# A list schedule with another order of dense tiles and other ranks, a gate taken chunk by chunk, and a tail in pairs

## The chip, the cores and the metric

The kernel runs on 1 core of one Trainium2 chip. The metric is the device time of one execution in microseconds (us); before the change it is 1162.19 us, the median of 3 runs (1161.91 to 1167.45). The engines are named as the profile names them: PE (TensorE), DVE (VectorE), ACT (ScalarE), POOL (GpSimd) and SP (SyncE, which here issues the DMAs).

## The reference, cut to what matters

Two layers work on 128 context tokens and 512 latent tokens of width 1024, all in float32. Layer 0 is a Conformer convolution branch, which the change does not touch. Layer 1 is a bidirectional Mamba-2 branch, and a final RMSNorm follows:

```python
u = h @ w_in
z, xbc, dt_raw = jnp.split(u, [SSD_INNER, SSD_INNER + XBC_DIM], axis=-1)
xbc = jax.nn.silu(depthwise_conv(xbc, w_conv, b_conv))
xs, bm, cm = jnp.split(xbc, [SSD_INNER, SSD_INNER + SSD_GROUPS * D_STATE], axis=-1)
dt_f = jax.nn.softplus(dtr_f + dt_bias_f.astype(f32))
...
y_f, s_f = ssd_scan(xs, dt_f, a_f, bm, cm, h0_f)
y_b, s_b = ssd_scan(flip(xs), flip(dt_b), a_b, flip(bm), flip(cm), h0_b)
y = y_f + flip(y_b) + d_skip.astype(f32)[:, None] * xs.astype(f32)
y = y.reshape(b, l, SSD_INNER) * jax.nn.silu(z.astype(f32))
y = rms_norm(y.reshape(b, l, SSD_GROUPS, SSD_INNER // SSD_GROUPS),
             norm_g.reshape(SSD_GROUPS, SSD_INNER // SSD_GROUPS)).reshape(b, l, SSD_INNER)
return y.astype(h.dtype) @ w_out, s_f, s_b
```

The scan runs in chunks of 128 tokens: chunk 0 holds the context tokens, chunks 1 to 4 the latent ones. The 32 heads lie in 4 groups, and the norm is taken over each group of 512 channels.

## The kernel before

Channels lie on the 128 partitions and the 640 tokens along a row. The tokens stand in two sides of 320 (64 of context and 256 of latent tokens each). Everything the change touches is in layer 1, and it is issued by a list scheduler written in the kernel, the class `Order`. Each piece of work is a Python generator, a chain, which yields operations with an engine and an assumed duration (`op`, `either`), waits for named results (`key`) or waits for a free buffer of a ring (`get`). At each step `run` takes the operation that could start earliest by the assumed clocks; ties go to the lower rank `prio`, then to the older chain. So the instruction order of all five engines is fixed when the program is built. On the chip each engine goes through its own row in that order and waits at semaphores.

**Dense tiles.** A projection tile is 8 k-blocks x 3 products (high and low halves of weights and activations) in two token halves, 48 matmuls. Its weights come by one DMA (`w_load`, L782), are rounded on ACT (`wh`, L786), and the remainder `wl` is made on DVE or POOL, whichever `either` favours (L790). Tiles are named here by letter, group and number. `x` tiles (16), `b` and `c` tiles (4 each) need the short convolution (`convolve`): the product leaves PSUM through one of two `up` buffers, then DVE makes four multiply-adds (L856) into one of three `xs` (or two `bc`) buffers, ACT takes the SiLU, and PE transposes into tokens (`to_tokens`, L879) in one of two `xt` buffers. `z` tiles (16) leave PSUM by ACT alone (L932) into the single `zs` buffer of their group. `o` tiles are the output products of groups 0 to 2 (`out2`). The tile products share two PSUM slots, `mm`. The chain `filler` takes the tiles in one fixed list; before, that list is x02 x03 b0 c0 x10 to x13, then group by group z tiles, b, c, x and o tiles, and the last group's products at the end.

**Groups.** `time_steps` turns the raw dt into softplus by a polynomial and into running sums, on DVE (L1391, L1394). `group` then runs the scan of a group chunk by chunk, in the order 4, 3, 2, 1, 0 (the last group 4, 3, 0, 2, 1): decays by DMA, POOL and DVE (`decay_half`), states (`chunk_state`), products (`py`, L1154), and y with the single `y` buffer, brought back to channels on PE (`pty`, L1113) and added on DVE (L1117). `norm` waits for all chunks of y, multiplies by the SiLU of z in 16 small DVE products per group (L1186), squares on ACT (L1197), sums on PE, takes the reciprocal root, scales (L1231) and splits into halves (`split_y`). Only then is the group's `zs` buffer free, and the group's `o` tiles can start.

**Tail.** The last group is normalised side by side (side 1 first). `last_products` makes 8 column tiles per side of 12 matmuls, each in its own `mm` slot; `last_residual` adds on DVE (L1280), squares on ACT and adds the squares up on DVE (L1290). `final` sums over the partitions (L177), takes root and reciprocal, spreads the result (L182), scales into `fo` buffers on DVE (L1331), and stores (L1336).

## Time and profile before

| | us |
|---|---|
| median of 3 runs (lowest, highest) | 1162.19 (1161.91, 1167.45) |
| the profiled execution | 1166.93 |
| its span, first to last instruction | 1165.0 |
| PE busy | 1083.9 |
| DVE busy | 845.9 |
| POOL busy | 562.9 |
| ACT busy | 557.7 |
| mean granted PE clock | 0.971 |

Layer 1's dense tiles start at about 595 us of the span. "Busy" counts an engine's instructions from start to end; a busy PE is one with a matmul in flight. In the rows of a timeline or of the chain, `x48` merges equal neighbours, the first number is the start and the second the time that the merged rows cover, and a bracket tells how long the engine stood idle before and what ended that. In a windows view, PEclk is the share of full speed that PE's clock was granted.

### The profile page before, as it was taken

How to read it: one execution, taken by the hardware profiler on the slowest of the kernel's cores; microseconds unless marked ns; L12 is line 12 of the kernel's file. 1: busy time of each engine (PE TensorE's matmuls, PEld its weight loads, DVE VectorE, ACT ScalarE, POOL GpSimd, SP SyncE). 2: the span in 40 equal slices, each digit the busy share in tenths (PEclk: the TensorE clock that was granted, in tenths of full speed). 3: DMA queues.
4: the chain of work that ended last, by engine and by line, in shares of the span. 5: the costliest groups of instructions: out<-in, count | busy, mean ns of one | idle time of the engine just before them, and what ended most of it. 6: DMA issues, size and time to landing. Idle time of an engine off the chain costs nothing. (4 is left out here: it accounts for less than half of the span.)

```text
span 1165.0 us, 18976 instructions
## 1 busy us (share of the span) xinstructions
PE 1083.9 (93%) x7548; PEld 985.5 (85%) x7548; DVE 845.9 (73%) x1234; ACT 557.7 (48%) x877; POOL 562.9 (48%) x467
## 2 busy tenths in 40 slices
PE   6999999998999999999986999988999999999886
PEld 3898888888998999999886978866899889988666
DVE  2588999899989499314768785798656975575776
ACT  6534447455554456212645655373257433562331
POOL 2156779777878448000020576626551565237410
PEclk9999999998998999999997999989999999999988
DMA  9343423341222112514222443423433343324202
GB/s 363 144 127 127 136 83 112 126 137 54 98 66 62 55 46 68 172 52 136 73 76 61 134 124 109 123 64 96 125 94 106 93 113 109 119 82 133 75 1 91
DMA packets 79047, 121.21 MB, mean 104 GB/s; under 512 B 5488, under 2 KB 49008, under 8 KB 78960
## 3 DMA queue, kind: packets, MB, share of 16 engines
q1 hardware_dynamic: 78960, 120.01, 32.9%
q8 instruction: 59, 0.97, 0.4%
q14 instruction: 28, 0.23, 0.1%
HBM read 115.07 MB, written 4.92 MB: 103 GB/s over the span
## 5 line engine op out<-in xcount | busy, mean ns | idle before, releaser
L361 DVE SCALAR_TENSOR_TENSOR cva<-v,cst,cva 128x550 f32<-128x550 f32 (+12 forms) x386 | 285.9, 814 | 10.2 <-ACT cva L354 8.7
L80 POOL TENSOR_TENSOR wl<-wf,wh 128x1024 fp32r<-128x1024 f32 (+1 forms) x50 | 119.1, 2383 | 124.8 <-ACT wh L78 120.0
L78 ACT CAST wh<-wf 128x1024 fp32r<-128x1024 f32 (+1 forms) x75 | 71.4, 955 | 185.1 <-PE o__4929 L148 37.4
L390 POOL TENSOR_TENSOR cv<-cv,tp 128x490 f32<-128x490 f32 (+3 forms) x94 | 113.7, 1213 | 13.7 <-ACT cv L388 9.4
L786 ACT CAST wh<-wf 128x1024 fp32r<-128x1024 f32 x53 | 55.6, 1048 | 97.6 <-issue 27.9
L824 PE MATMUL o<-yhl,wh 128*128 128x320 f32 x384 | 98.9, 345 | 0.0
L790 DVE TENSOR_TENSOR wl<-wf,wh 128x1024 fp32r<-128x1024 f32 x49 | 70.0, 1428 | 29.1 <-ACT wh L786 29.0
L824 PE MATMUL pz<-h_hi,wh 128*128 128x384 f32 (+1 forms) x256 | 88.4, 345 | 1.2 <-ACT zs L933 1.2
L385 ACT ACTIVATE tp<-v,cst 128x490 f32<-128x490 f32 (+3 forms) x94 | 65.7, 715 | 40.7 <-POOL cv L390 40.6
L1094 POOL TENSOR_TENSOR y<-y,yo 128x512 f32<-128x512 f32 x32 | 48.6, 1518 | 67.6 <-DVE yo L1092 67.5
L824 PE MATMUL pz<-h_hi,wl 128*128 128x384 f32 (+1 forms) x256 | 79.2, 309 | 0.0
L824 PE MATMUL pz<-h_lo,wh 128*128 128x384 f32 (+1 forms) x256 | 79.1, 309 | 0.0
L824 PEld LDWEIGHTS o<-yhl,wh 128*128 128x128 f32 x384 | 66.2, 192 | 13.6 <-issue 13.3
L824 PE MATMUL xs<-h_hi,wh 128*128 128x384 f32 (+1 forms) x224 | 73.3, 327 | 4.8 <-ACT up L843 4.8
L856 DVE SCALAR_TENSOR_TENSOR xs<-up,cst,xs 128x642 f32<-128x642 f32 x64 | 72.4, 1136 | 6.2 <-ACT xs L854 5.3
L80 DVE TENSOR_TENSOR wl<-wf,wh 128x512 fp32r<-128x512 f32 (+1 forms) x25 | 27.2, 1086 | 67.6 <-ACT wh L78 67.5
L969 POOL TENSOR_TENSOR gb<-gb,cols 128x512 f32<-128x512 f32 x40 | 48.5, 1212 | 45.8 <-DMA gb<-acd 36.4
L824 PE MATMUL xs<-h_hi,wl 128*128 128x384 f32 (+1 forms) x224 | 70.0, 312 | 0.0
L824 PE MATMUL xs<-h_lo,wh 128*128 128x384 f32 (+1 forms) x224 | 69.9, 312 | 0.0
L969 POOL TENSOR_TENSOR gf<-gf,cols 128x512 f32<-128x512 f32 x40 | 51.5, 1288 | 36.1 <-DMA gf<-acd 36.1
L824 PE MATMUL o<-yhl,wl 128*128 128x320 f32 x192 | 60.2, 314 | 0.0
L628 POOL MEMSET up<- 128x2 f32 x2 | 0.2, 100 | 118.5 <-DVE h_lo L219 118.5
(678 smaller groups left out, 3469.4 us busy)
## 6 DMA issues: line engine op xcount, KB each, us to landing
wf<-w_in SPq DMA_DIRECT2D x48, 512.0 KB, 3.6
wa<-w_ada SPq DMA_DIRECT2D x64, 256.0 KB, 4.7
wf<-w_out SPq DMA_DIRECT2D x24, 512.0 KB, 3.7
wf<-w_xbc SPq DMA_DIRECT2D x24, 512.0 KB, 3.7
gf<-acd SPq DMA_DIRECT2D x40, 256.0 KB, 4.6
gb<-acd SPq DMA_DIRECT2D x40, 256.0 KB, 4.5
wa<-w_ada SPq DMA_DIRECT2D x16, 512.0 KB, 9.9
wf<-w_z SPq DMA_DIRECT2D x16, 512.0 KB, 3.8
```

Of the source, the lines that this page charges most:

```text
L78: S.copy(out=wh[:, :n], in_=wf[:, :n])
L80: sub.tensor_sub(out=wl[:, :n], in0=wf[:, :n], in1=wh[:, :n].bitcast(F32))
L361: V.scalar_tensor_tensor(out=rows(acc)[:, :, lo:hi], in0=rows(v)[:, :, lo + d : hi + d], scalar=w_dw(i, tap), in1=rows(acc)[:, :, lo:hi], ...
L385: S.activation(out=tp[:, :, 0 : hi - lo], in_=rows(v)[:, :, lo + d : hi + d], func=AF.Copy, scale=w_dw(i, tap))
L390: G.tensor_add(out=rows(out)[:, :, lo:hi], in0=rows(out)[:, :, lo:hi], in1=tp[:, :, 0 : hi - lo])
L628: G.memset(t[:, 0:2], 0.0)
L786: S.copy(out=cell["wh"], in_=cell["wf"])
L790: e_.tensor_sub(out=cell["wl"], in0=cell["wf"], in1=cell["wh"].bitcast(F32))
L824: T.matmul(ps[:, b, at_ : at_ + t1 - t0], lhsT=w_, rhs=t_[:, t0:t1], start=k == 0 and n == 0, stop=k == nk - 1 and n == 2)
L856: t = yield op(VE, 0.95, lambda: V.scalar_tensor_tensor(out=acc, in0=u[:, d : d + PW], scalar=c("w_c", j * 5 + d), in1=acc, op0=ALU.mult, ...
L969: yield op(PO, 1.15, lambda: G.tensor_sub(out=gt, in0=gt, in1=cols1[ch][:, o : o + 4].unsqueeze(2).broadcast_to([P, 4, 128])))
L1094: t = yield op(PO, 1.35, lambda: G.tensor_add(out=y, in0=y, in1=yo))
```

## The change

- **Order of the tiles.** The list of `filler` is written out as a string, `PLAN`. `z` tiles stand early and between the `x` tiles: z00 first, then x02, b0, c0, x10, x03, z01 and so on. The `x` tiles of groups 2 and 3 and the `o` tiles are spread.
- **Ranks.** `start` takes its rank from a table by the chain's name, `PRIO`, in place of a number at each call. `either` gets its own bias in place of a common one, and an `up` buffer is taken by the time at which it came free, not in turn.
- **Gate by chunk.** The 16 products of `norm` become one product per chunk and group (L1191 of the changed kernel, 5 per group, 512 elements each), in chains of their own, `gate`, which start as soon as the chunk's y and the four z tiles are there. The squares may go to ACT or to DVE.
- **y buffers.** From the third chunk of the last group on, y has two further buffers, which come free when the last projection tile is done.
- **Tail.** Two column tiles share one `mm` slot; the last products wait for the residuals of group 2 and are chains with ranks of their own. The squares of columns 1 to 5 are added up on POOL, and those of columns 6 and 7 go to the partition sum as they are. `final` works in three overlapping parts of 128 tokens (one root, one reciprocal), scales in place in `x` and stores from there.
- **Series.** In `time_steps` the factors 1/17 and 2 of the polynomial are moved into the multiply-adds, and two TENSOR_SCALAR instructions are gone. The logarithm starts earlier in the chain.

```diff
-                            key = (t + 0.4 * load if len(ch[4][1]) == 1 else t + dur - 1.25 + 2.0 * n, ch[2], ch[3])
+                            key = (t + 0.4 * load if len(ways) == 1 else t + dur - ways[0][1] + bias * n, ch[2], ch[3])
...
+        PRIO = {"x_after": 2, "filler": 3, "decay_half": 3, "decay_state": 1, "chain0": 0, "chain1": 0, "other_y": -3, "copy_y": -1, "split_y": -1, "groups": 0, "decays": -1, "norms": -3, "gate": 3, "products1": 3, "products0": 2, "residual0": 1, "final0": -2, "w_chain": 0, "time_steps": 1, "columns": 0, "logarithm": 0, "rows_out": 0, "ends_out": 1, "weights_out": 0, "first_steps": 0, "b_after": -2, "c_after": 0, "z_after": 2, "split": 3, "add_residual": 2, "out_weights": 1, "free_bc": -1, "final1": 3, "prompt": -3, "residual1": 0, "store": -1}
...
-            u = up[ups[0] % 2]
-            ups[0] += 1
+            ups.sort()
+            u = up[ups.pop(0)[1]]
...
+                ring = "y" if g < 3 or n < 2 else "y3"
+                yield get(ring)
...
+        def gate(g, ch):
+            yield key(("y", g, ch), *[("z", g, j) for j in range(4)])
+            zv = halves4(grp[g]["zt"])
+            zv = zv[:, :, :, 0:64] if ch == 0 else zv[:, :, (ch - 1) // 2, 64 + (ch - 1) % 2 * 128 : 192 + (ch - 1) % 2 * 128]
+            yv = grp[g]["xt"][:, ch, :]
+            yv = yv.rearrange("p (j b n) -> p j b n", j=4, b=2) if ch == 0 else yv.rearrange("p (j n) -> p j n", j=4)
+            t = yield op(VE, 0.68, lambda: V.tensor_mul(out=zv, in0=zv, in1=yv))
+            post(("gate", g, ch), t)
...
-            yield key(*[("y", g, ch) for ch in chs])
+            yield key(*[("gate", g, ch) for ch in chs])
...
-                t = yield op(VE, 0.45, lambda: V.tensor_add(out=accs[b][0], in0=accs[b][0], in1=sq))
-                put("xs", t)
+                t = yield op(PO, 0.85, lambda: G.tensor_add(out=accs[b][0], in0=accs[b][0], in1=sq))
+                put(nm, t)
...
-        PARTS = ((0, 128), (128, 128), (256, 64))
+        PARTS = ((0, 128), (128, 128), (192, 128))
...
-                yield get("st")
-                o = lp.tile([P, 512], F32, tag="st", bufs=6, name="fo")[:, 0:HN]
-                t = yield op(VE, 0.5, lambda: V.scalar_tensor_tensor(out=o, in0=x[k][:, tok], scalar=c("fg", k), in1=cell[0], op0=ALU.mult, op1=ALU.mult))
-                start(store(k, tok, o), t, 1)
+                t = yield op(VE, 0.54, lambda: V.scalar_tensor_tensor(out=x[k][:, tok], in0=x[k][:, tok], scalar=c("fg", k), in1=cell[0], op0=ALU.mult, op1=ALU.mult))
+                start(store(k, tok), t)
...
+        PLAN = "z00 x02 b0 c0 x10 x03 z01 x11 x12 z02 b1 x20 x21 z03 x13 x30 x22 x31 c1 z10 b2 z11 x23 x32 c2 o00 o01 o02 x33 z12 z13 o03 b3 z20 z21 o10 c3 o11 z22 z23 o12 z30 o13 z31 o20 z32 z33 o21 o22 o23"
...
-            yield tts(0.36, V.tensor_scalar, out=u, in0=t, scalar1=1.0 / 17, scalar2=None, op0=ALU.mult)
             for n in (15, 13, 11, 9, 7, 5, 3):
-                yield stt_(out=u, in0=u, scalar=1.0 / n, in1=t, op0=ALU.add, op1=ALU.mult)
-            yield tts(0.36, V.tensor_scalar, out=u, in0=u, scalar1=1.0, scalar2=2.0, op0=ALU.add, op1=ALU.mult)
-            yield tts(0.5, V.tensor_mul, out=q, in0=q, in1=u)
+                yield stt_(out=u, in0=t if n == 15 else u, scalar=17.0 / n, in1=t, op0=ALU.add, op1=ALU.mult)
+            yield stt_(out=q, in0=u, scalar=17.0, in1=q, op0=ALU.add, op1=ALU.mult)
```

What the change moves is seen in the order of the instructions on each engine. The first place is the start of layer 1's tiles on PE: `pt<-cst,v` are the transposes of the end product v of `time_steps`, `xs` and `B` are tiles. Before:

```order
L824 MATMUL xs<-h_lo,wh 128x256
L824 MATMUL xs<-h_hi,wl 128x256
L1462 MATMUL pt<-cst,v 128x128 x3
L1462 MATMUL pt<-cst,t 128x128 x3
L824 MATMUL B<-h_hi,wh 128x384
L824 MATMUL B<-h_lo,wh 128x384
```

And now, at the same transposes:

```order
L827 MATMUL B<-h_hi,wh 128x256
L827 MATMUL B<-h_lo,wh 128x256
L827 MATMUL B<-h_hi,wl 128x256
L1460 MATMUL pt<-cst,v 128x128 x3
L827 MATMUL B<-h_hi,wh 128x256
```

Ahead of the transposes of v stood two tiles (x02, x03); now two tiles (z00, x02) and 30 of b0's 48 matmuls stand there. On DVE, the polynomial at the same place, before:

```order
L1394 TENSOR_SCALAR q<-e 128x384
L1394 RECIPROCAL q<-q 128x384
L1394 TENSOR_TENSOR t<-e,q 128x384
L1394 TENSOR_TENSOR t<-t 128x384
L1394 TENSOR_SCALAR u<-t 128x384
L1391 SCALAR_TENSOR_TENSOR u<-u,t 128x384 x7
L1394 TENSOR_SCALAR u<-u 128x384
L1394 TENSOR_TENSOR q<-q,u 128x384
```

and now:

```order
L1396 TENSOR_SCALAR q<-e 128x384
L1396 RECIPROCAL q<-q 128x384
L1396 TENSOR_TENSOR t<-e,q 128x384
L1396 TENSOR_TENSOR t<-t 128x384
L1393 SCALAR_TENSOR_TENSOR u<-t 128x384
L1393 SCALAR_TENSOR_TENSOR u<-u,t 128x384 x6
L1393 SCALAR_TENSOR_TENSOR q<-u,q 128x384
```

The two TENSOR_SCALAR rows on u are gone. Beside this chain POOL makes the remainders `wl` of the next tiles' weights: three of them before the first decay before, five now; DVE made two just ahead of it before, one now.

The second place is DVE after the last chunks of group 0's y (`xt<-xt,pty`). Before, the convolution of B and C stands around the gate `zs<-zs,xt`, whose 16 rows follow each other (four of them shown):

```order
L790 TENSOR_TENSOR wl<-wf,wh 128x1024
L856 SCALAR_TENSOR_TENSOR C<-up_5971,cst,C 128x642 x2
L970 COPY_PREDICATED gf<-msk,gb 128x512
L1117 TENSOR_TENSOR xt<-xt,pty 128x512
L856 SCALAR_TENSOR_TENSOR B<-up_5967,cst,B 128x642
L1186 TENSOR_TENSOR zs<-zs,xt 128x64
L1186 TENSOR_TENSOR zs<-zs,xt 128x256
L1186 TENSOR_TENSOR zs<-zs,xt 128x64
L1186 TENSOR_TENSOR zs<-zs,xt 128x256
```

and now, where three of the five gate rows already stand further up:

```order
L1133 TENSOR_TENSOR xt<-xt,pty 128x512
L1161 TENSOR_TENSOR gf<-gf,pcb 128x512
L869 SCALAR_TENSOR_TENSOR xs<-up_5971,cst,xs 128x642 x4
L869 SCALAR_TENSOR_TENSOR B<-up_5967,cst,B 128x642 x3
L1133 TENSOR_TENSOR xt<-xt,pty 128x512
L869 SCALAR_TENSOR_TENSOR B<-up_5967,cst,B 128x642
L1191 TENSOR_TENSOR zs<-zs,xt 128x8x64
L1191 TENSOR_TENSOR zs<-zs,xt 128x4x128
L793 TENSOR_TENSOR wl<-wf,wh 128x1024
```

Between the last y of group 0 and the first y of group 1, DVE had 22 rows of convolution (16 for x, 4 for B, 2 for C), 16 of gate and 4 remainders; it now has 13 (8, 1, 4), 2 and 5. PE had 246 dense matmuls there and now has 267.

The third place is the end of PE's row: `o` are the last products, `rps<-ones,sq` the sums of squares, `rps<-cst,rc` the spreading. Before:

```order
L1308 MATMUL o_11246<-yhl,wh_10896 128x320 x2
L1308 MATMUL o_11246<-yhl,wl_10897 128x320
L177 MATMUL rps<-ones,sq 128x1 x4
L177 MATMUL rps<-ones,sq 64x1 x2
L182 MATMUL rps<-cst,rc 128x128 x2
L182 MATMUL rps<-cst,rc 128x64
```

and now:

```order
L1329 MATMUL o_11136<-yhl,wl_10959 128x320
L1329 MATMUL o_11136<-yhl,wh_10958 128x320 x2
L1329 MATMUL o_11136<-yhl,wl_10959 128x320
L177 MATMUL rps<-ones,sq 128x1 x18
L182 MATMUL rps<-cst,rc 128x128 x6
```

Side 1's sums, spread and scaling stood among side 0's products; now those of both sides stand behind the last product, and DVE scales and SP stores all 16 pieces after it. Further up in the tail, 120 dense matmuls stand between the last y that side 1 needs and its first product (48 before), and 135 between the last y of side 0 and its first product (90 before).

More of the change, by code (lines that the diff above doesn't have):

```diff
@@ L753, in op, with either @@
             return "op", ((eng, dur, fn, table),)
[L755 to L756 removed]
+        def either(*ways, bias=2.0):
+            return "op", tuple((e_, d_, f_, None) for e_, d_, f_ in ways), bias
         def key(*ks):
@@ L802, in w_load @@
             t = yield op(SP, 0.1, load)
-            start(split(), t, 1)
+            start(split(), t)
         W = {}
@@ L1323, in final @@
-            for p, cols in ((P, slice(0, 2)), (64, slice(2, 3))):
-                yield op(ACT, 0.26, lambda: S.activation(out=rc[0:p, cols], in_=ps[0:p, 384:387][:, cols], func=AF.Sqrt, scale=1.0 / 1024, bias=epsb[0:p]), "sqrt")
-                yield op(VE, 0.16, lambda: V.reciprocal(out=rc[0:p, cols], in_=rc[0:p, cols]))
+            t = yield op(PE, 1.0, lambda: column_sums(ps[:, 384:387], accs[b], PARTS))
+            for _ in range(3):
+                put(SQ[b][0], t)
+            rc = gp.tile([P, 3], F32, tag="rc", bufs=1, name="rc")
@@ L1326, in final @@
+            yield op(ACT, 0.26, lambda: S.activation(out=rc, in_=ps[:, 384:387], func=AF.Sqrt, scale=1.0 / 1024, bias=epsb), "sqrt")
+            yield op(VE, 0.16, lambda: V.reciprocal(out=rc, in_=rc))
             cell = []
```

224 lines of the change are left out of this document (104 added, 120 removed).

## The prediction

> **What bounds the kernel now.** First the page's head and its row of engines:
>
> ```profile
> span 1165.0 us, 18976 instructions
> PE 1083.9 (93%) x7548; PEld 985.5 (85%) x7548; DVE 845.9 (73%) x1234; ACT 557.7 (48%) x877; POOL 562.9 (48%) x467
> ```
>
> PE is busy for 93% of the span, so the question is where the other 7% lie. The change touches layer 1, from 595 us on; the windows view cuts that into stretches (length, then busy time of PE, PEld, DVE, ACT, POOL, then granted clock, DMA share, GB/s):
>
> ```profile
> 595.00:640.00 45.00, 32.29 (x197) 31.15 (x196) 39.68 (x53) 22.37 (x37) 8.92 (x4) 0.81 0.28 82
> 640.00:740.00 100.00, 98.87 (x661) 88.76 (x659) 72.86 (x87) 58.59 (x86) 63.99 (x46) 1.00 0.42 123
> 740.00:815.00 75.00, 63.83 (x412) 54.72 (x411) 66.82 (x93) 39.65 (x68) 38.62 (x29) 0.91 0.30 90
> 815.00:1085.00 270.00, 268.40 (x1827) 242.33 (x1826) 177.39 (x283) 121.29 (x189) 129.06 (x105) 1.00 0.37 108
> 1085.00:1154.00 69.00, 58.86 (x362) 48.46 (x360) 50.56 (x115) 24.90 (x47) 15.29 (x11) 0.93 0.13 40
> 1154.00:1165.00 11.00, 2.42 (x18) 2.09 (x18) 5.13 (x13) 0.87 (x3) 0.00 (x0) 0.70 0.34 119
> ```
>
> In 640 to 740 and 815 to 1085 PE idles 1.1 + 1.6 = 2.7 of 370 us at full clock: nothing to gain. PE loses in three places: the start (idle 12.7, clock 0.81), the change from group 0 to 1 (idle 11.2, clock 0.91) and the tail (idle 10.1, clock 0.93), and behind the last product come 11 us with little PE work. A low clock stretches work: (1 - 0.81) x 45 = 8.6, 0.09 x 75 = 6.8 and 0.07 x 69 = 4.8 us. The list of waits names who ends PE's idle time there (us, times, longest):
>
> ```profile
> PE pt L1462 <- DVE v L1394: 11.3, 1, 11.3
> PE py L1154 <- DVE gf L1145: 4.2, 3, 2.7
> PE xs L824 <- ACT up L843: 3.5, 1, 3.5
> PE rms L1221 <- DVE rq L1213: 3.3, 1, 3.3
> PE rms L1207 <- ACT ysq L1197: 1.9, 2, 1.0
> PE o L1308 <- DVE x L1280: 1.9, 3, 0.8
> ```
>
> So DVE, at 89% in the second stretch (66.82 of 75), is late while PE has nothing else in its row.
>
> **Start.** PE's timeline around the one long wait, and a whole tile from the chain:
>
> ```profile
> 608.61 0.28 PE L824 MATMUL xs<-h_hi,wl 128*128 128x256 f32 x1
> 620.19 0.88 PE L1462 MATMUL pt<-cst,v 128*128 128x128 f32 x3 [11.30 <-DVE v L1394]
> 621.74 0.90 PE L1462 MATMUL pt<-cst,t 128*128 128x128 f32 x3 [0.67 <-DVE t L1452]
> 623.38 0.69 PE L824 MATMUL B<-h_hi,wh 128*128 128x384 f32 x1 [0.73 <-ACT up L843]
> 1001.56 7.03 PE B L824 x48
> ```
>
> Of b0's 48 matmuls 30 now stand ahead of v's transposes: 30/48 x 7.03 = 4.4 us of work that fills part of the 11.3. A tile is a tile, so z00 in place of x03 is nothing by itself; but a z tile needs no `up` buffer, so B's wait of 0.73 for ACT's move into `up` goes; I leave the 0.67 for t. The shorter idle time also costs less low clock. Against this stands when v is ready. DVE's and POOL's timelines:
>
> ```profile
> 599.20 0.35 DVE L1394 TENSOR_SCALAR q<-e 128x384 f32<-128x384 f32 x1
> 603.36 2.44 DVE L1394 TENSOR_SCALAR u<-t 128x384 f32<-128x384 f32 x1
> 605.83 4.11 DVE L1391 SCALAR_TENSOR_TENSOR u<-u,t 128x384 f32<-128x384 f32 x7
> 609.98 2.50 DVE L1394 TENSOR_SCALAR u<-u 128x384 f32<-128x384 f32 x1
> 619.49 0.56 DVE L1394 TENSOR_TENSOR v<-rp,v 128x384 f32<-128x384 f32 x1
> ```
>
> ```profile
> 602.91 2.67 POOL L790 TENSOR_TENSOR wl<-wf,wh 128x1024 fp32r<-128x1024 f32 x1 [0.76 <-ACT wh L786]
> 609.93 2.34 POOL L790 TENSOR_TENSOR wl<-wf,wh 128x1024 fp32r<-128x1024 f32 x1 [4.35 <-ACT wh L786]
> ```
>
> The two instructions that go took 2.44 + 2.50, yet their sister of the same size took 0.35. Each ended just after a remainder on POOL: 605.80 after 605.58, 612.48 after 612.27. So 2 x 2.1 of their 4.9 us were time under POOL, and their own worth is 0.7. If the next instruction is held in their stead, v comes 0.7 earlier; if none is, 4.9 (2.44 + 2.50). POOL now makes five remainders there, not three, so v can also come later, by one or two more such blocks of 2.1; DVE makes one remainder less. I take v as before: gain 4.4 + 0.7 and 0.9 for the clock = **6**, with bounds 2 (two more blocks) and 15 (4.9 earlier, and half of the low clock's 8.6 back).
>
> The Trainium skill, "SBUF — State Buffer", section "Who interferes with whom", says that a DVE instruction with two SBUF inputs contends with a GpSimd instruction that reads SBUF, and that the holder blocks the other for its whole duration. By that rule the multiply-adds, whose inputs are both in SBUF, would be held like the scalar steps, and the larger number of remainders on POOL would speak against the change. The trace agrees for the two 2.4 us rows. By that rule the time would be that of the second rival below, not that of the sum.
>
> **Group 0 to group 1.** DVE's timeline from the last gate to the last split, with the groups by line over layer 1 and a later 128x512 product of that kind:
>
> ```profile
> 747.63 8.61 DVE L1186 TENSOR_TENSOR zs<-zs,xt 128x64 f32<-128x64 f32 x16
> 756.17 0.88 DVE L856 SCALAR_TENSOR_TENSOR B<-up,cst,B 128x642 f32<-128x642 f32 x1
> ...
> 795.51 0.48 DVE L1244 TENSOR_TENSOR yhl<-zs,yhl 128x320 fp32r<-128x320 f32 x1
> ...
> 814.36 0.69 DVE L1117 TENSOR_TENSOR xt<-xt,pty 128x512 f32<-128x512 f32 x1
> ```
>
> ```profile
> L856 DVE SCALAR_TENSOR_TENSOR xs<-up,cst,xs 128x642 f32<-128x642 f32 x64 | 72.4, 1136 | 6.2 <-ACT xs L854 5.3
> L790 DVE TENSOR_TENSOR wl<-wf,wh 128x1024 fp32r<-128x1024 f32 x48 | 68.7, 1432 | 28.7 <-ACT wh L786 28.5
> ```
>
> The old gate held DVE for 8.6 us in one piece. Now five products, at 0.69 by the 128x512 row: 3.4, three of them earlier. Between the last y of group 0 and the first y of group 1 DVE loses 9 convolution rows (9 x 1.14 = 10.2), 14 gate rows (8.61 - 2 x 0.69 = 7.2) and gains one remainder (1.4): **16 us less work**, where PE was idle or slowed for 11.2 + 6.8 = 18. PE's own row gains 21 dense matmuls there (21/48 x 7.03 = 3.1), which are work taken from elsewhere, and cover. Since the shortfall and the relief are alike, I take **15**; bounds 5 (only the 4.2 of `gf` and the low clock that it brings go) and 18 (all).
>
> **Tail.** PE waits there for `rq`, `ysq` and x: 3.3 + 1.9 + 1.9 = 7.1 of the idle 10.1. Between the last y and the first product of side 1 stand 120 dense matmuls in place of 48, of side 0 135 in place of 90: 72/48 x 7.03 = 10.5 and 6.6 us more cover, over norm chains whose waits are 3.3 and 1.9. Tiles in pairs leave DVE two tiles' time per slot, so the 1.9 for x go. Those 7.1, 1.1 of the remaining idle 3.0, and the low clock's 4.8 make **13**; bounds 6 (only `rq` and the pairs' half) and 15.
>
> **End.** After the last product:
>
> ```profile
> 1153.67 0.31 PE L1308 MATMUL o<-yhl,wl 128*128 128x320 f32 x1
> 1154.61 0.48 DVE L1290 TENSOR_TENSOR sq<-sq 128x320 f32<-128x320 f32 x1
> 1155.14 1.38 PE L177 MATMUL rps<-ones,sq 128*128 128x1 f32 x12 [1.17 <-DVE sq L1290]
> 1157.16 1.04 PE L182 MATMUL rps<-cst,rc 128*128 128x128 f32 x6 [0.64 <-DVE rc L1325]
> 1158.24 3.76 DVE L1331 SCALAR_TENSOR_TENSOR fo<-x,cst,rps 128x320 f32<-128x320 f32 x8 [1.09 <-PE rps L182]
> 1158.82 3.78 SPq L1336 DMA_DIRECT2D o_y<-fo  x8
> ```
>
> (The trace counts two records for one of these matmuls.) 6 sums took 1.38; 18 take 4.1, of which 1.2 fit into PE's wait for the residual and 0.5 replaces the last add: +1.1. Eight more scalings and stores at 3.78/8 follow one another: +3.8. The second side's spread hides behind the first side's scaling. **Cost 5**, bounds 3 (all sums hidden) and 7 (none, and the spread too). The adds of squares on POOL have no row: at least the 0.48 of DVE's, at most the 2.67 of a remainder three times as long. At five or six per side, 32 us at most, beside POOL's 15.29 busy of 69, they cost nothing while products cover them; the last two columns skip the add.
>
> The remaining edits (choice of `up` buffer, `either`'s bias, further y buffers) show only in the order just counted. Their risk is new stalls in the 370 full us; PE has 2.7 us of idle time there, and DVE's 72.86 in 100 and 177.39 in 270 leave it room, so I put it at 0, up to 5.
>
> **Sum.** 6 + 15 + 13 - 5 = 29. The profiled execution's own time is 1166.9, 4.7 above the median; 1166.9 - 29 = 1138 stands for a run like it, and 1162.2 - 29 = **1133** for the median, which I predict. A difference of 0.5%, 5.8 us, is about what a measurement of this kernel can tell from no change.
>
> **Rivals.**
>
> *v is not held* (0.13). The removed steps were the ones that POOL's remainders caught; if the multiply-adds slip through, the start gains 15: 1133 - 9 = 1124. For: the seven took 4.11, 0.59 each, though part of one remainder's span lay near. Against: five remainders in place of three.
>
> *POOL holds DVE more* (0.17). Layer 1 gives POOL six more remainders and ten adds of squares. v comes two blocks later (start 2), and half the relief between the groups is eaten: 1133 + 4 + 7.5 = 1145. For: the two 2.4 us rows. Against: 6 x 2.1 = 13 us over the whole layer, most of it where DVE has slack. (The Trainium skill's rule quoted above leads here.)
>
> *Nothing gained* (0.08). The idle time only moves to the next late piece: gains under 10 us before the end's cost of 5, so 1157 to 1168. For: DVE's 89% in the second stretch; against: its work falls there.
>
> *Slower* (0.08). Group 1's first two z tiles now stand among group 0's; the next two need the single `zs` buffer only when norm has split group 0, and each occupies one of two `mm` slots until ACT moves it out. If the split is late, both slots are held and PE starves. From group 0's last y to there PE has 228 dense matmuls (33.4 us) and about 8 of other work, 42 us; before, the last gate to the last split took 756.2 to 796.0 = 39.8. With the 16 us of relief the split needs some 24, so it would decide only beyond 42; each us beyond is lost at three group changes. At 58 us (16 over, 48 lost, 29 gained) the time is 1181.
>
> **How the numbers follow.** Forecast (1126 to 1141) 0.54, v not held 0.13, POOL holds 0.17, nothing gained 0.08, slower 0.08. Low: all upper bounds, 6 → 15, 15 → 18, 13 → 15 and 5 → 3, make 45 or 1117; a little beyond, 1114, as the groups 1 to 3 may gain too. High: 2 + 5 + 6 - 7 = 6 gives 1156; I end at 1154, leaving out the cases without a gain. Faster by over 0.5% is the first three cases and a part of the fourth's edge: 0.85; within 0.5% 0.07; slower 0.08.
>
> **What would show it.** Right: PE's gap before `pt<-cst,v` is near 6 us; no window between 720 and 800 has a clock under 0.95; PE's waits for `rq`, `ysq` and x are under 2 us together; from the last product to the end 15 to 16 us, with 16 stores in a row. Wrong: v's last product later than 20.3 us after `q<-e` (619.49 - 599.20 before); long multiply-adds beside POOL's remainders; a wait of `pz` for ACT's move into `zs`, which would be the slower case; or new idle time in the full stretches.

## The result, and the profile after

The changed kernel takes 1145.32 us (median of 4 runs, 1144.77 to 1151.12) beside 1163.55 us for the kernel before: a ratio of 0.985, with a 95% interval from 0.9808 to 0.9892. Forecast were 1133 us and a range from 1114 to 1154. The time lies in the range and fell as forecast, but by 18 us in place of 29.

To see where the 18 us lie, both profiled executions are cut into stretches in which PE does the same work (35, 83, 72 and 247 us of matmuls, each counted with the usual distance between the starts of two matmuls of its shape, then the rest up to the last product, then the end). The lengths can then be compared row by row, to about 1 us: so much depends on where exactly the cuts lie. The windows view before, cut in this way:

```profile
594.50:646.00 51.50, 38.75 (x239) 37.61 (x240) 43.95 (x58) 26.88 (x45) 11.74 (x6) 0.83 0.29 85
646.00:732.00 86.00, 84.87 (x566) 75.24 (x565) 63.74 (x76) 52.57 (x76) 54.66 (x41) 1.00 0.42 123
732.00:825.00 93.00, 81.83 (x529) 70.44 (x529) 77.58 (x109) 44.49 (x76) 52.95 (x39) 0.93 0.32 94
825.00:1082.00 257.00, 255.41 (x1741) 231.13 (x1740) 170.25 (x269) 117.86 (x184) 118.91 (x95) 1.00 0.37 107
1082.00:1154.00 72.00, 61.86 (x383) 51.46 (x381) 52.16 (x118) 25.48 (x48) 17.62 (x13) 0.93 0.16 48
1154.00:1165.00 11.00, 2.42 (x18) 2.09 (x18) 5.13 (x13) 0.87 (x3) 0.00 (x0) 0.70 0.34 119
```

And after:

```profile
590.90:635.00 44.10, 36.98 (x234) 36.60 (x235) 41.05 (x49) 25.50 (x39) 12.25 (x5) 0.88 0.29 81
635.00:719.00 84.00, 84.00 (x562) 76.92 (x561) 59.14 (x69) 43.61 (x73) 47.31 (x37) 1.00 0.41 125
719.00:799.00 80.00, 76.15 (x529) 68.77 (x528) 72.61 (x88) 48.52 (x79) 40.15 (x29) 1.00 0.31 93
799.00:1064.00 265.00, 259.48 (x1762) 228.65 (x1761) 193.80 (x281) 128.64 (x195) 154.81 (x122) 0.99 0.39 116
1064.00:1126.10 62.10, 55.99 (x356) 46.95 (x355) 36.34 (x74) 20.55 (x40) 19.58 (x18) 1.00 0.06 18
1126.10:1144.00 17.90, 8.44 (x49) 7.85 (x47) 8.36 (x20) 1.00 (x3) 0.00 (x0) 0.57 0.41 147
```

Layer 1, from its first product to the last instruction, takes 553.1 us in place of 570.5. The first, third and fifth stretch are shorter by 7.4, 13.0 and 9.9 us. The fourth, where PE was full before, is longer by 8.0 us: PE idles there 5.5 us (265.00 less 259.48) in place of 1.6, at a clock of 0.99 in place of 1.00, and DVE and POOL are busier by 24 and 36 us. So about half of the 8.0 us is idle time; the rest lies in matmuls that stand further apart than usual. The end is longer by 6.9 us. In all that is 7.4 + 2.0 + 13.0 - 8.0 + 9.9 - 6.9 = 17.4 us; the fifth stretch holds 2.2 us less of PE's work, sums and spreads that stand in the end now.

PE's waits after, in layer 1, largest first, show what is late now (`gf` is a tile of decays, `stn` one of states, `rq` and `ysq` belong to the norm):

```profile
PE pt L1460 <- DVE v L1396: 7.1, 1, 7.1
PE o L1329 <- DVE x L1299: 6.1, 13, 0.8
PE pty L1129 <- POOL y L1108: 4.3, 3, 1.5
PE po L1102 <- DVE stn L1067: 2.3, 1, 2.3
...
PE pz L827 <- ACT zs L947: 1.2, 1, 1.2
```

The 11.3 before v's transposes fell to 7.1, and the waits for `gf`, `rq` and `ysq` are gone. New are 13 waits of the last products for x, three for y from POOL, and one of 2.3 for `stn`. DVE at the start, where the series is computed:

```profile
594.23 0.35 DVE L1396 TENSOR_SCALAR q<-e 128x384 f32<-128x384 f32 x1
...
598.04 2.64 DVE L1396 TENSOR_TENSOR t<-t 128x384 f32<-128x384 f32 x1
...
601.31 5.61 DVE L1393 SCALAR_TENSOR_TENSOR u<-u,t 128x384 f32<-128x384 f32 x6
...
610.74 4.09 DVE L1396 TENSOR_TENSOR_SCAN rp<-one,q 64x384 f32<-64x384 f32 x2
...
616.62 0.56 DVE L1396 TENSOR_TENSOR v<-rp,v 128x384 f32<-128x384 f32 x1
```

and POOL beside it:

```profile
595.19 5.07 POOL L793 TENSOR_TENSOR wl<-wf,wh 128x1024 fp32r<-128x1024 f32 x2 [12.99 <-ACT wh L789]
602.28 2.44 POOL L793 TENSOR_TENSOR wl<-wf,wh 128x1024 fp32r<-128x1024 f32 x1 [2.02 <-ACT wh L789]
610.70 2.34 POOL L793 TENSOR_TENSOR wl<-wf,wh 128x1024 fp32r<-128x1024 f32 x1 [5.97 <-ACT wh L789]
```

The square t, which took 0.56 before, took 2.64 here; the six multiply-adds took 5.61 (six at 0.59 are 3.5), the two scans 4.09 (1.93 before). That is three times some 2.1 us, each where a remainder runs on POOL. The RECIPROCAL that runs beside the first of them took 2.55, as it does without one. From the start of `q<-e` to the start of v's last product it takes 22.4 us (20.3 before), and to its end 22.9: the two scalar steps are gone, and three other instructions are held in their place.

At the end, behind the last product:

```profile
1125.98 5.42 PE L177 MATMUL rps<-ones,sq 128*128 128x1 f32 x36
...
1131.27 1.63 PE L182 MATMUL rps<-cst,rc 128*128 128x128 f32 x6
...
1133.32 7.42 DVE L1350 SCALAR_TENSOR_TENSOR x<-x,cst,rps 128x320 f32<-128x320 f32 x16
1133.45 1.65 PE L182 MATMUL rps<-cst,rc 128*128 128x128 f32 x6 [0.56 <-DVE rc L1346]
1133.86 7.75 SPq L1355 DMA_DIRECT2D o_y<-x  x16
```

The first spread begins only behind all 18 sums (36 records, 5.42 us), and 16 scalings and 16 stores follow in one row. The granted clock was 1.00 from 1126.1 to 1128.0 us and 0.57 from 1128.0 to 1131.4; the records of the sums follow each other by 0.11 us up to 1128.4 and by 0.21 from 1128.5 on.

### The profile page after: what moved, and what is told of

Read it like the earlier page. It is cut to its first block, busy times and chain, and to the rows that moved or that the text cites. A ratio compares the mean times of both kernels' runs of the same rounds, so it can differ in the third digit from the quotient of the medians.

```text
span 1144.0 us, 18912 instructions
## 1 busy us (share of the span) xinstructions
PE 1076.4 (94%) x7560; PEld 979.3 (86%) x7560; DVE 844.4 (74%) x1170; ACT 557.3 (49%) x873; POOL 580.7 (51%) x483
## 4 chain that ended last, share of the span: by engine, by line
PE 70%; DVE 17%; ACT 5%; issue 3%; DMA 2%; POOL 2%; SPq 1%; DVEq 0%; POOLq 0%; ACTq 0%
PE xs L827 7%; PE pz L827 7%; PE o L827 6%; PE o L1329 3%; DVE cva L361 3%; PE po L1102 2%; PE C L827 2%; PE pst L1039 2%; DVE cn L524 2%; PE py L1170 2%; ACT wh L78 2%; DVE yhl L1262 1%; PE o__5398 L148 1%; PE o__4929 L148 1%; PE o__4927 L148 1%
## 5 line engine op out<-in xcount | busy, mean ns | idle before, releaser
L827 PE MATMUL o<-yhl,wh 128*128 128x320 f32 x384 | 93.4, 330 | 0.0
L869 DVE SCALAR_TENSOR_TENSOR xs<-up,cst,xs 128x642 f32<-128x642 f32 x64 | 74.1, 1158 | 14.4 <-ACT xs L867 13.2
L827 PE MATMUL xs<-h_hi,wh 128*128 128x384 f32 (+1 forms) x224 | 76.0, 339 | 0.0
L793 DVE TENSOR_TENSOR wl<-wf,wh 128x1024 fp32r<-128x1024 f32 x43 | 57.5, 1338 | 18.4 <-ACT wh L789 18.2
L983 POOL TENSOR_TENSOR gf<-gf,cols 128x512 f32<-128x512 f32 x40 | 50.2, 1255 | 28.0 <-DMA gf<-acd 26.3
```

What stands on the lines that cost most here:

```text
L793: e_.tensor_sub(out=cell["wl"], in0=cell["wf"], in1=cell["wh"].bitcast(F32))
L827: T.matmul(ps[:, b, at_ : at_ + t1 - t0], lhsT=w_, rhs=t_[:, t0:t1], start=k == 0 and n == 0, stop=k == nk - 1 and n == 2)
L869: t = yield op(VE, 0.95, lambda: V.scalar_tensor_tensor(out=acc, in0=u[:, d : d + PW], scalar=c("w_c", j * 5 + d), in1=acc, op0=ALU.mult, ...
L983: yield op(PO, 1.15, lambda: G.tensor_sub(out=gt, in0=gt, in1=cols1[ch][:, o : o + 4].unsqueeze(2).broadcast_to([P, 4, 128])))
```

## The experiments

How small edits are read: layer 0 has the same order of PE's, DVE's and POOL's instructions in all kernels, yet layer 1 begins between 589.0 and 594.5 us in these profiles. The changed kernel profiled a second time had layer 1 in 553.0 us (553.1 the first time), although it began 2.9 us later. So the length of layer 1 in the profile is given for every run, beside the median of its times. Differences under 1 us are not read even so: in the eight profiles here that have the changed kernel's 126 matmuls ahead of v's transposes, and v at the same time, the 200th matmul stands 38.1 to 39.0 us after layer 1's start, since the clock stays low behind the gap for v for a different time. "Lost" is a stretch's length less PE's work in it, for stretches of equal work: before 16.3 (start), 2.9, 20.9 (group 0 to 1), 10.1 (full stretch), 22.1 (tail); after 9.5, 1.0, 7.6, 18.1, 14.4.

| run | median us | ratio to before, 95% interval | layer 1, us |
|---|---|---|---|
| before | 1161.96 to 1163.55 | 1 | 570.5 |
| changed | 1145.32 | 0.985, 0.9808 to 0.9892 | 553.1 |
| changed, again | 1147.13 | 0.9871, 0.9851 to 0.989 | 553.0 |
| residuals after the pair | 1140.88 | 0.9805, 0.9781 to 0.983 | 546.0 |
| side 1's end early | 1141.01 | 0.9808, 0.9783 to 0.9833 | 548.7 |
| both | 1143.65 | 0.9827, 0.9804 to 0.9849 | 549.3 |
| remainders of POOL set to zero | 1131.91 | 0.9729, 0.9708 to 0.9751 | 539.1 |
| old gate | 1150.30 | 0.9897, 0.9879 to 0.9916 | 556.6 |
| old list | 1175.62 | 1.0123, 1.0103 to 1.0143 | 583.5 |
| two steps back | 1150.93 | 0.9915, 0.9883 to 0.9947 | 557.5 |
| all remainders on DVE | 1154.84 | 0.9939, 0.9918 to 0.9959 | 561.4 |
| later remainders on DVE | 1137.76 | 0.9798, 0.978 to 0.9817 | 545.4 |
| the same, residuals after the pair | 1134.03 | 0.9769, 0.975 to 0.9787 | 540.7 |
| old ranks | 1150.42 | 0.9908, 0.9883 to 0.9932 | 556.0 |

**The tail's pairs.** The loop over the two halves starts the residuals behind the products:

```diff
-                    start(last_residual(b, 2 * mp + j, ps, left), t, f"residual{b}")
+                for j in range(2):
+                    start(last_residual(b, 2 * mp + j, pair[:, j, 0:HN], left), t, f"residual{b}")
```

> The changed kernel, but the residuals of both halves of a pair of last products are issued after the products of both halves; before that the first half's residual stood between the products of the second half. Theory (one tile, one owner): PE and DVE hand the one PSUM tile of a pair back and forth although they touch different halves, and this makes PE's 13 waits for x (6.1 us idle, 8.3 us with the restarts). Then these waits go, to under 1 us in all, the last residuals come about 0.8 us later, and the time falls by 6 to 8 us, to 1138. Rival (DVE is late with the residuals): the waits only move to the start of the next pair and stay above 4 us; 1143 to 1147.

PE and DVE in the changed kernel, within one pair (the bracket gives the idle time and who ended it):

```profile
1118.02 0.31 PE L1329 MATMUL o<-yhl,wl 128*128 128x320 f32 x1
1118.37 0.28 DVE L1299 SCALAR_TENSOR_TENSOR x<-o,mod,x 128x64 f32<-128x64 f32 x1 [1.52 <-PE o L1329]
1118.71 0.56 PE L1329 MATMUL o<-yhl,wh 128*128 128x320 f32 x2 [0.38 <-DVE x L1299]
1119.11 0.31 PE L1329 MATMUL o<-yhl,wl 128*128 128x320 f32 x1
1119.45 0.48 DVE L1299 SCALAR_TENSOR_TENSOR x<-o,mod,x 128x256 f32<-128x256 f32 x1 [0.80 <-PE o L1329]
1119.99 0.56 PE L1329 MATMUL o<-yhl,wh 128*128 128x320 f32 x2 [0.58 <-DVE x L1299]
```

PE ends the first half, DVE reads 64 columns of it, PE makes three matmuls of the second half, DVE reads 256 columns, PE goes on: each waits for the other, though no column is shared. After the edit the waits for x in the whole tail are one:

```profile
PE o L1329 <- DVE x L1299: 1.6, 1, 1.6
```

The theory holds, though the waits are not quite under 1 us; "DVE is late" falls, since DVE does the same work. The tail loses 9.2 us in place of 14.4, and layer 1 is 7.1 us shorter, of which some 0.8 lie in the start, which the edit does not touch. The median moved by less than was expected, by 4.4 us to 1140.88; the five runs lie between 1136.34 and 1144.03.

**The end.** One rank:

```diff
-"final1": 3
+"final1": 1
```

> The changed kernel with the rank of side 1's end (sums, spread, scaling, stores) raised, so that it stands among side 0's products as it did before the change. Theory (the end is too long by side 1's half): from the last product to the end it takes 11 to 13 us in place of 18.1, PE's row before it grows by the 9 sums and 3 spreads of side 1 (about 3.5 us): 2 to 3 us faster, 1143. Rival (the eight scalings on DVE then make side 0's residuals late): PE's waits for x grow by the eight scalings' 3.8 us or more, and the time is 1145 to 1148.

Behind the last product stand the sums of side 0 alone (18 records, the last 14 shown), and then half the stores:

```profile
1128.42 1.72 PE L177 MATMUL rps<-ones,sq 128*128 128x1 f32 x14 [0.99 <-ACT sq L1306]
...
1132.39 3.76 DVE L1350 SCALAR_TENSOR_TENSOR x<-x,cst,rps 128x320 f32<-128x320 f32 x8 [1.74 <-PE rps L182]
1132.96 3.78 SPq L1355 DMA_DIRECT2D o_y<-x  x8
```

The end takes 12.0 us in place of 17.9, and layer 1 is 4.4 us shorter, more than expected: side 1's sums and spreads, which PE makes ahead of the last product now, partly fill waits for x (8 waits and 3.6 us are left of 13 and 6.1). They have a price that was not expected: behind the row of side 1's sums the granted clock was 0.50 for 5.3 us (1110.5 to 1115.8), and three products of the other side took 0.80 us there in place of 0.44. Then both edits at once:

> Both edits of the tail together: residuals after the whole pair, and side 1's end among side 0's products. If both theories hold and don't share a cause, the gains add: 1145 - 7 - 2.5 = 1135.5 (1133 to 1138). If the end of side 1 has no room beside the residuals once PE runs without its waits: 1138 to 1141.

The gains did not add up, and the second range (1138 to 1141) was missed too, by 2.7 us. Layer 1 took 549.3 us, 3.3 more than with the residuals alone (546.0) and no less than with the early end alone (548.7). PE, now faster, is at the last product when DVE still scales side 1 in one row of eight (3.76 us); the residuals of side 0 come behind it, and PE waits 3.0 us for the sums of squares before its own sums. The granted clock is low behind side 1's sums here too (0.57 from 1117 to 1121 us). So side 1's early end needs the time that the false waits gave.

**Remainders on POOL.**

```diff
+            def clear():
+                cell["wl"] = gp.tile([P, 1024], F32R, tag="wl", bufs=3, name="wl")
+                G.memset(cell["wl"].bitcast(F32), 0.0)
...
-                t = yield either((VE, 1.25, lambda: low(V)), (PO, 2.45, lambda: low(G)))
+                t = yield either((VE, 1.25, lambda: low(V)), (PO, 2.45, lambda: clear()))
```

> The changed kernel, in which the ten weight remainders that POOL makes in layer 1 are set to zero in place of being computed (the small part of ten tiles' products is left out): POOL's instruction then writes but reads nothing, and the order on the other four engines is the same. Theory (POOL's reading remainder holds DVE's two-input instructions): the three lengthened rows at the start (t 2.64, one multiply-add 2.6, one scan about 3.1 us) fall to 0.56, 0.56 and 0.97, v comes 6 us earlier, PE's gap before v's transposes falls from 7.1 to 1 or 2, and DVE's rows in the full stretch that lie beside a remainder fall too: 1145 - 6 - 2 = 1137 (1133 to 1140). Rival (the rows are long for another reason, such as the engine's own pipeline or the weights' transfers): rows and gap stay, 1144 to 1147.

The same DVE rows with POOL writing only:

```profile
597.09 0.56 DVE L1400 TENSOR_TENSOR t<-t 128x384 f32<-128x384 f32 x1
597.68 0.56 DVE L1397 SCALAR_TENSOR_TENSOR u<-t 128x384 f32<-128x384 f32 x1
598.28 3.52 DVE L1397 SCALAR_TENSOR_TENSOR u<-u,t 128x384 f32<-128x384 f32 x6
...
605.10 0.73 DVE L1400 TENSOR_SCALAR q<-e,an 128x384 f32<-128x384 f32 x1
605.93 1.94 DVE L1400 TENSOR_TENSOR_SCAN rp<-one,q 64x384 f32<-64x384 f32 x2
```

```profile
597.57 0.95 POOL L797 MEMSET wl<- 128x1024 f32 x1 [7.84 <-PE pz L831]
604.66 0.96 POOL L797 MEMSET wl<- 128x1024 f32 x1 [6.14 <-PE xs L831]
```

All three lengthened rows are back at 0.56, 3.5 and 1.94; `u<-t` lies beside a MEMSET for its whole length, the scans have none beside them. PE's gap for v is 0.9 us. The start loses 0.5 us in place of 9.5, which is more than v's 6.3: the granted clock is 1.00 over the whole start, where it was 0.72 from 609 to 618 us (the gap) and 0.50 from 618 to 622 behind it. The change of groups loses 5.2 (7.6), the full stretch 14.6 (18.1). Layer 1 is 14 us shorter, at the same order on PE, DVE and ACT, and the median of 1131.91 lies below the theory's range: the 2 us that were counted for all that is not v were too few. The instruction is shorter too (0.95), so for the two later stretches this run does not tell holding from POOL's own lateness; at the start the rows themselves do. The Trainium skill, "SBUF — State Buffer", section "Who interferes with whom", has a two-input DVE instruction contend with GpSimd's reads and not with its writes; the 0.56 beside a MEMSET agrees, and so do the 2.64 beside a remainder.

So could DVE make the remainders itself?

```diff
-                t = yield either((VE, 1.25, lambda: low(V)), (PO, 2.45, lambda: low(G)))
+                t = yield op(VE, 1.25, lambda: low(V))
```

> The changed kernel with all weight remainders of layer 1 on DVE, none on POOL; the schedule is worked out anew. Theory (a remainder on POOL costs DVE about 2.1 us of standing still where it meets a two-input instruction, more than the 1.2 us that it takes on DVE itself): v comes about 2.5 us earlier, the new gaps in the full stretch shrink, and the time is 1140 (1136 to 1143). Rival (DVE is the engine without room, and ten more remainders there are 12 us): 1148 to 1156.

With no POOL instruction beside them, the square took 0.56, the six multiply-adds 3.53 and the scans 1.94. v did come 6.5 us earlier after layer 1's start, and the full stretch lost 11.4 us in place of 18.1. But DVE makes the next remainders only behind v (from 615.22 us), the schedule put only 48 matmuls of one tile ahead of v's transposes, and PE's gap there was 12.5 us, with a further 5.1 for an `up` buffer. The start lost 19.4. The theory's mechanism showed and its time did not. The time, 1154.84, lies in the rival's range, but its reason (DVE full) is not what was seen: the full stretch, where DVE works longest, became shorter, and the loss lies at the start and at the change of groups (about 12.5 lost in place of 7.6). With the choice left to the schedule for the first seven tiles, which keeps the five early remainders on POOL:

```diff
-                t = yield either((VE, 1.25, lambda: low(V)), (PO, 2.45, lambda: low(G)))
+                t = yield either((VE, 1.25, lambda: low(V)), (PO, 2.45, lambda: low(G))) if i < 7 else op(VE, 1.25, lambda: low(V))
```

> The changed kernel, in which the five early remainders stay on POOL and the five later ones (in the full stretch and the tail) are made on DVE; the schedule is worked out anew from the first of them on. Theory (the later remainders on POOL hold DVE in the full stretch, and that makes part of its new gaps): the gaps of the stretch from 800 to 1065 us fall from 5.5 us of idle time to under 3, the start stays (7.1 us gap), and the time is 1142 (1139 to 1145). Rival (the gaps come from the row in which the schedule puts PE's transposes and products, which any new schedule draws again): gaps stay or move to other waits, 1144 to 1151.

Layer 1 in 545.4 us, and a median of 1137.76, below the theory's range: the full stretch loses 13.1 in place of 18.1 and the change of groups 5.5 in place of 7.6, the start as before. The wait of 2.3 for `stn` is gone, those for y stay, and one of 1.8 for `gf` is new; PE's idle time there fell from 5.5 only to 4.0 us (260.00 less 256.02 in this row of its windows view), not to under 3. So waits both went and moved, as the theory and the rival each said, and the gain cannot be divided between the two:

```profile
795.00:1055.00 260.00, 256.02 (x1755) 226.81 (x1754) 201.18 (x286) 127.70 (x191) 151.57 (x119) 1.00 0.41 120
```

With the residuals behind the pair as well:

> The same, and the residuals of a pair issued after both its halves. If the two causes are separate, the gain of the residuals (7 us from layer 1's first product to the end) comes on top: 1136 (1133 to 1139). If not, it stays at 1139 to 1145.

Both gains add up: 540.7 us, and 1134.03 us for the whole, a ratio of 0.9769 (0.975 to 0.9787) beside 0.9871 (0.9851 to 0.989) for the changed kernel run in the same call. Only the run whose remainders POOL sets to zero, and so leaves out, is faster.

**Gate, list, series, ranks.** The old gate (5 chunk products replaced by the 16 rows in `norm`, `xt` freed behind them):

```diff
-            t = yield op(VE, 0.68, lambda: V.tensor_mul(out=zv, in0=zv, in1=yv))
-            post(("gate", g, ch), t)
+            post(("gate", g, ch), run.keys["y", g, ch])
...
+            for j in range(4):
+                for b in sides:
+                    for z_, yv, d_ in (
...
+                        t = yield op(VE, d_, lambda: V.tensor_mul(out=z_, in0=z_, in1=yv))
```

> The changed kernel with the old gate: 16 small products per group on DVE in one piece, after all of the group's y, in place of one product per chunk as its y comes; list of tiles and ranks stay as changed, the schedule is worked out anew. Theory (gate and list share the gain between the groups): DVE's 8.6 us piece comes back before each norm in place of 3.4 us spread out, 5.2 us per group, which costs PE 4 to 6 us at the change from group 0 to 1 and 1 to 2 us at each later one: 1145 + 8 = 1153 (1149 to 1157). Rival (the list alone made the gain, since PE has cover there now): 1144 to 1148.

Layer 1 is 3.5 us longer: 4.5 at the change from group 0 to 1 (12.1 lost in place of 7.6), and at the later groups nothing is lost (18.6 beside 18.1). The theory has the right place, but not the reason: at group 0 the piece took 3.84 us and not 8.6.

```profile
755.96 3.84 DVE L1212 TENSOR_TENSOR zs<-zs,xt 128x64 f32<-128x64 f32 x16
759.73 3.02 DVE L869 SCALAR_TENSOR_TENSOR B<-up,cst,B 128x642 f32<-128x642 f32 x1
```

Before the change four of the 16 rows stood beside POOL's instructions and took 1.06, 2.43, 1.27 and 1.06 us, 5.82 in all; the same rows without POOL take 0.21 or 0.41, 1.05 in all. So 4.8 of the 8.61 us were time under POOL. Of POOL's four rows there, the first three of which follow, only one is a remainder; the others are decays:

```profile
747.96 1.13 POOL L969 TENSOR_TENSOR gb<-gb,cols 128x512 f32<-128x512 f32 x1 [2.94 <-DMA gb<-acd]
749.38 2.39 POOL L790 TENSOR_TENSOR wl<-wf,wh 128x1024 fp32r<-128x1024 f32 x1 [0.29 <-ACT wh L786]
751.73 1.04 POOL L969 TENSOR_TENSOR gf<-gf,cols 128x512 f32<-128x512 f32 x1
```

With the old gate in the new schedule POOL was held in its turn: a remainder that began beside the gate took 5.22 us, and the convolution of B behind the gate 3.02 (0.88 for the one ahead of it). So the 4.5 us are not the price of a longer gate, and the run of the series, below, shows that a new schedule alone can draw as much.

The old list:

```diff
-        PLAN = "z00 x02 b0 c0 x10 x03 z01 x11 x12 z02 b1 x20 x21 z03 x13 ...
+        PLAN = "x02 x03 b0 c0 x10 x11 x12 x13 z00 z01 z02 z03 b1 c1 x20 x21 ...
```

> The changed kernel with the tiles in the order of the list before (x02 x03 b0 c0 x10 to x13, then group by group); gate by chunk, ranks, tail and series stay as changed. Theory (the list carries the start and its share between the groups): no b0 matmuls ahead of v's transposes, so PE's gap there is 11 us or more again (+5 to 7), and between group 0 and 1 the x and c convolutions stand before y again (+6 to 8): 1145 + 13 = 1158 (1153 to 1163). Rival (the gate carries the change between the groups): only the start is lost, 1150 to 1152.

30 us, more than twice the 13 that were expected: with the old list the other edits are slower than the kernel before. The start loses 15.3, the change of groups 26.6, and the tail 26.4. PE's waits between the groups:

```profile
PE rms L1239 <- DVE zs L1249: 4.0, 1, 4.0
PE py L1170 <- DVE gf L1161: 3.4, 1, 3.4
PE po L1102 <- DVE stn L1067: 2.5, 1, 2.5
```

The series:

```diff
+            yield tts(0.36, V.tensor_scalar, out=u, in0=t, scalar1=1.0 / 17, scalar2=None, op0=ALU.mult)
             for n in (15, 13, 11, 9, 7, 5, 3):
-                yield stt_(out=u, in0=t if n == 15 else u, scalar=17.0 / n, in1=t, op0=ALU.add, op1=ALU.mult)
-            yield stt_(out=q, in0=u, scalar=17.0, in1=q, op0=ALU.add, op1=ALU.mult)
+                yield stt_(out=u, in0=u, scalar=1.0 / n, in1=t, op0=ALU.add, op1=ALU.mult)
+            yield tts(0.36, V.tensor_scalar, out=u, in0=u, scalar1=1.0, scalar2=17.0, op0=ALU.add, op1=ALU.mult)
+            yield tts(0.56, V.tensor_mul, out=q, in0=q, in1=u)
```

> The changed kernel with the two scalar steps put back into the series. Theory (a remainder on POOL holds whichever DVE instruction comes next, so the steps' own worth was 0.35 us each): from the start of the instruction q<-e to v's last product it takes 22.9 us now and 23.6 (23.0 to 24.2) then; the time is 1145 to 1148. Rival (the steps themselves took 2.4 and 2.5): 27 to 28 us, and the time is 1150.

From `q<-e` to the end of v's last product it took 23.4 us (22.9 without the steps), and each step took 0.36: on v's way they are worth half a microsecond. Yet layer 1 is 4.5 us longer, and the time is the rival's figure for a reason that neither named: the start loses 8.7 (9.5 without the steps), while the three stretches from there to the tail lose 5.1 more. The schedule, which reckons in assumed times, moved several hundred of PE's 3480 matmuls of layer 1 for that half microsecond. So an edit ahead of the middle can draw a few microseconds there anew, and the 3 to 5 us of the runs with a new schedule are to be read with that.

The old ranks (the table replaced by the numbers that the calls had before):

> The changed kernel with the chains' ranks of before the change; list, gate by chunk, tail in pairs and series stay as changed. Theory (list and gate carry the gain, ranks only settle ties): the gap at the start stays near 7 us and the change between the groups under 10 us lost; side 1's end stands among side 0's products again, as in the run that raised its rank, and the time is 1140 to 1149. Rival (the list is only good with these ranks): new waits of several us between the groups, 1153 to 1170.

Layer 1 in 556.0 us; the median lies just above the theory's range and below the rival's. The start is better by 2.5 us and the end by 5.4 (side 1's end stands early again); the change of groups is worse by 4.1 and the full stretch by 2.9. These do not price the ranks alone, since with them `either` gives POOL four remainders in place of ten. Only two of them run beside the series, two of its rows are held (2.21 for 0.56, 5.60 for 3.5), and v comes 3.3 us earlier.

The changed kernel again:

> The changed kernel once more, on the chip of this call, for the comparison with the edits: a ratio to the kernel before of 0.985, between 0.983 and 0.988.

The ratio is 0.9871, inside that range, and layer 1 took 553.0 us. No run takes back the choice of the `up` buffer, the bias of `either`, the further y buffers, the adds on POOL or the pairs themselves, so their shares stay open.

## Why the prediction was right, and where its sum was not

- **Start: 6 forecast, 6.8 measured.** b0's matmuls fill the gap as reckoned. That the next instruction is held in place of a removed step was right, and not only as a chance: three others were held. The chain from `q<-e` to v became 2.1 us longer by that, and began 1.4 us earlier after layer 1's start, behind one remainder less on DVE. So v's transposes begin 0.7 us later (26.3 us after layer 1's start beside 25.7), which "as before" covers. The rival "v is not held" fell. What the prediction took for the low clock (8.6) counts the idle time too: of the 16.3 us lost in the start, 12.7 were idle, so the clock had cost 3.6 at most. Only a bound used it.
- **Group 0 to 1: 15 forecast, 13.3 measured.** The relief of DVE was the right reason: between the last y of group 0 and the first y of group 1 DVE was busy for 60.7 us of 68.2 before and for 46.0 of 55.4 now, 14.7 us less, where 16 were counted; and with the old list PE waits for DVE there again (`zs`, `gf`, `stn`). Of the 7.2 us that were counted for the gate, 4.8 had been time under POOL and not the gate's own work. The parts are not additive: undoing the gate costs 4.5 us there, which a new schedule alone can cost, undoing the list 19.0.
- **Tail: 13 forecast, 7.7 measured** (the lost time, 22.1 to 14.4; a further 2.2 of work moved behind the last product and is in the end). `rq` and `ysq` are gone from the waits, as the added cover was to do. Of the 13, idle time was to give 8.2 and gave 4.0 (10.1 to 6.1); the clock was to give 4.8, and all else that was lost fell by 3.7, with the clock at 1.00 in place of 0.93. The step that failed is "Tiles in pairs leave DVE two tiles' time per slot, so the 1.9 for x go". They became 6.1 us in 13 waits. The order showed the residual's rows between the products of one tile; what was missed is that PE and DVE wait for each other over the whole tile and not per half. The run with residuals behind the pair shows it.
- **End: cost 5 forecast, 6.9 measured.** The failed step is "The second side's spread hides behind the first side's scaling": the first side's spread stood behind all 18 sums, which took 5.42 and not 4.1 (the 4.1 reckons with the time of sums at a clock of 1.00; it was 0.57 in the later ones), and scaling began 7.2 us behind the last product (1126.15 to 1133.32; 4.3 before). That is 2.9 us more, where 1.1 were counted; the eight further scalings cost 3.7, as forecast.
- **Full stretches: 0 forecast, up to 5; 8.0 lost in the long one, 1.9 gained in the short one.** The failed step is that DVE's room (177.39 of 270) makes new stalls unlikely. PE's new waits there are for y and `stn`, single instructions late by 1 to 2 us. Moving five remainders from POOL to DVE gives back 5.0 us. How much of that is holding, how much POOL's own queue and how much the new schedule, stays open: the run without reading says 3.5 for the first two together.

The rival "POOL holds DVE more" named 1145, and that is the time measured, but not by its sum: it wanted the start at 2 and half the relief between the groups eaten. Both gains came nearly whole, so that its time fits is luck. Its cause is real: rows of DVE are held beside POOL's remainders in both kernels. What that costs was measured in the changed one alone, 14 us for holding and POOL's own time together. One reading of the prediction goes too far: the Trainium skill's rule that it quotes speaks of two inputs in SBUF, and the two rows of 2.4 us (`u<-t`, `u<-u`) have one. The seven multiply-adds, which have two, ran in a pause of POOL (605.83 to 609.94, between remainders that ended at 605.58 and began at 609.93), so they told nothing about the rival. The two-input rows that were held before the change stand in the 8.61 us of the gate, which the prediction shows and takes for the gate's own work. The slower rival did not come near: PE waits for the move into `zs` for 1.2 us, once, as it did before the change.

The signs that were named beforehand came out mixed. As for a right forecast: a gap of 7.1 us before v's transposes (near 6), a clock of 1.00 from 720 to 800 us, and 16 stores in a row. As for a wrong one: v's last product 22.4 us after `q<-e` (over 20.3), multiply-adds lengthened beside a remainder, and new idle time in the full stretch; also, the waits for x are 6.1 us where `rq`, `ysq` and x were to stay under 2 together, and the end is 17.9 us in place of 15 to 16. The time lies in the wide range and outside the likeliest band, 1126 to 1141: two of the gains were forecast well, and the tail, the end and the full stretch were not.

## What to carry to other kernels

In a schedule written out from assumed times, price an edit first by the gap that it fills, then ask what the new order puts next to what: the long instructions on POOL beside a chain on DVE cost more here (9 us at the start) than the two instructions that were removed. Look for every tile that two engines use in turns: halves of one tile are one tile to the waits. And compare stretches of equal work, not of equal time, or the gains of one stage hide the losses of the next.

## What the runs showed of the hardware

- A 128x1024 remainder on POOL (2.34 to 2.67 us) lengthened a DVE instruction beside it by about 2.1 us, whether scalar step (2.44 and 2.50 in place of 0.35), product (2.64 for 0.56), multiply-add (5.61 for 3.5 over six) or scan (4.09 for 1.94 over two). It also lengthened a row of the old gate (2.43 for 0.22), and POOL's decays (128x512, 1.04 to 1.22 us) lengthened others by about 0.85 each. A RECIPROCAL beside a remainder was not lengthened (2.55 with and without). It goes the other way too: a remainder that began beside the 16 rows of the old gate took 5.22 us. A MEMSET of the same tile (0.95) left two-input instructions at 0.56; the scalar step that met one took 0.73 in place of 0.42.
- PE's clock made the gap for v dearer than the gap itself: with v 6.3 us earlier the start lost 9.0 us less. The granted clock was 0.50 in the 4 us behind the gap and 0.84 in the next 4; without the gap it was 1.00 throughout.
- Behind a row of 9 or 18 sums (128x1 matmuls) the granted clock fell to 0.50 to 0.57, though PE was busy all the time: for 3.4 us within the 18 sums of the changed kernel, and for 5.3 us among the products that follow side 1's 9 sums in the run with the early end. Behind the 6 sums of the kernel before it stayed at 1.00 (1140 to 1145 us).
- Layer 1 repeated within 0.1 us between two profiles of one kernel (its start alone by 0.3), while layer 0 in the same order of instructions ended up to 4.8 us apart (589.0 to 593.8 among the changed kernels).
